# When the output weights of layer 0's attention are read and cut, and where the first output product and head 7's joins stand

## The chip, the cores and the metric

One core of one Trainium2 chip runs the whole program. The metric is device time in microseconds (us) of one execution, the median of several. Names of the engines: PE is TensorE (matrix products and transposes), PEld its weight loads, DVE is VectorE, ACT is ScalarE, POOL is GpSimd (nearly unused here), and SP only issues transfers (DMAs); SPq marks these issues. A `DMA_DIRECT2D` row is one issue; its transfer lands some microseconds later.

## The reference: what is computed

A decoder of two layers on x of 1024 tokens by 1024 columns, all in float32. Layer 0 mixes tokens by softmax attention in three groups of windows, layer 1 by gated linear attention; behind each stands an MLP with squared relu. The change lies in the end of layer 0's attention:

```python
def dilated_attention(h, w_in, w_out):
    qkv = (h @ w_in).reshape(B, S, N_GROUPS, 3, ATTN_HEADS, HEAD_DIM)
    for g, (window, dil) in enumerate(DILATED_GROUPS):   # 3 groups, 8 heads of 128
        q = apply_rope(qkv[:, :, g, 0], cos, sin) * (HEAD_DIM ** -0.5)
        k = apply_rope(qkv[:, :, g, 1], cos, sin)
        v = qkv[:, :, g, 2].astype(jnp.float32)
        o_g, lse_g = dilated_group_attention(q, k, v, dil, window // dil)
...
    alpha = jax.nn.softmax(jnp.stack(lses, axis=0), axis=0)
    o = jnp.sum(alpha[..., None] * jnp.stack(outs, axis=0), axis=0)
    return o.reshape(B, S, ATTN_WIDTH).astype(h.dtype) @ w_out
...
        x = x + dilated_attention(h, attn_w_in[j], attn_w_out[j])
```

Each head's three group outputs are merged by weights from the softmax denominators (here called a join); the eight heads side by side are multiplied by `w_out` (the output product), and x is added.

## The kernel before, in words

**Products.** Float32 matrices are held as two parts, a rounded high part and the rest (names ending in h or hi, and in l or lo). `mm3` (line 212) makes one product from three matmuls: high by high (L213), high by rest (L214), rest by high (L215). ACT casts the high part, and DVE subtracts it to get the rest (L222 for operands, L151 and L152 for weights).

**Weights.** The queue `W` holds the output product's weights in pieces of 128 by 1024 (512 KB) in the order in which they are needed. `W.dma()` (L132, its transfer L135) issues the load of the next piece (tile raw); `W.prep()` casts it (ACT `whi`, L151) and takes the rest (DVE `wlo`, L152). `W.pump()` (line 161) loads up to four pieces ahead and casts at most two of them, as long as `W.limit` plus the number of pieces given back lies above the number of casts. A piece needs a buffer of pool k4 (25 buffers) for raw, whi and wlo each.

**Attention.** There are 24 units p of one head and one group each, head by head. `run_head(p)` makes unit p's products (tiles pX, pY, pZ, pV) in 14 half products and calls `advance()` behind each: a clock goes on by one step, and all that `at(clock, function, rank)` has put down for that step is issued, in the order of the ranks. So `advance()` is what lays other work between products; the engines' queues then run in the order of issue. Unit p's rotary step is DVE work: c is added up from a bank (L1070), its halves are swapped by two copies (cw<-c, L1071 and L1072), and L1079, L1080 and L1087 give qT or kT. The attention of unit p runs while unit p + 1's products do: `scores` (PE pS, L976), `soft` (DVE L990, ACT's exponentials pt, L992), `turn` (PE's transposes pP, L1003, and ACT's copy L1005), `values` (PE pO, L1017). The result (orow) goes to a scratch og in HBM (L1024 or L1027).

**Joins.** `merge_load` reads the three groups' results of one head and of half of the tokens (rows, L1150). `merge_weights` and `merge` are DVE work (L1157 to L1175) and end in the tile om. Heads 0 to 6 write om to a scratch `oscr` in HBM, from where the output product's operand comes back: ol (heads 0 to 3, L1235) and ol2 (heads 4 to 6, L1434). Head 7's om is transposed by PE straight away (`t_head`, pT, L1218). Every operand is transposed (pT) and cut: heads 0 to 3 into oTh and oTl, heads 4 to 7 into o1h and o1l.

**The end of the attention.** With p = 23, the last unit, the output product's first four weights and ol are loaded and cast by hand-set clocks (c is the clock at the unit's start; lines 1406 to 1413). The last unit's own attention has no products of a following unit to stand between; `tail()` (line 1423) sets down its steps, the loads of ol2, the transposes of heads 4 to 6 and head 7's two joins by clock, advances three steps and leaves 40 more in the list `steps`.

**The output product.** `out_proj(0, ...)` (line 1448) runs over the 8 blocks of 128 tokens and 2 halves of the columns, first with the weights of heads 0 to 3, then with those of heads 4 to 7. `add_block` makes 12 matmuls into one of PE's 8 banks (pd), adds the residual xs (DVE, L1468) and calls `tick()`. In this stage each `tick()` takes two entries from `steps` and calls `W.pump()`:

```python
            xx = xs[tb // 2][:, tb % 2, 512 * n:512 * n + 512]
            dve.tensor_tensor(xx, ps, xx, op=OP.add)
            if quiet:
                W.pump()
            else:
                tick()
```

So a block of `add_block` is two steps of the clock, and what `tail()` has set down stands between the blocks.

Of the kernel before, what the change touches and what calls it, by code (L numbers as in the profile page):

```python
# [22 lines left out]
NB = S // P  # L23
# [18 lines left out]
def hybrid_trunk(ctx, tc, x, norm_mix, norm_mlp, norm_fin, a_in, a_out, g_in, g_up, g_b, g_nw,  # L42
# [32 lines left out]
    steps = deque()  # L75
# [104 lines left out]
    W = Weights()  # L180
# [104 lines left out]
    class Split:  # L285
# [4 lines left out]
        @staticmethod  # L290
        def at(tiles, k):
            n = 4 // len(tiles)
            return tiles[k // n][:, k % n, :]
# [11 lines left out]
    class Halves:  # L305
# [108 lines left out]
        def finish(self):  # L414
            up, a = self.up, self.a
            P1, P2, P6, P5, P7, P4, P3 = range(7)

            def split(name, src, lo):
                for c in range(2):
                    self.split(name, src, c, self.one, lo)  # L420

            up.product(0, P1)
            self.sum2(0)
            up.done(0, P1)
            up.first_stage(2)
            up.product(0, P2)
            up.stage(0, 3)
            up.product(1, P1)
            self.turn(3)
            up.first_stage(3)  # L430
            up.product(1, P2)
            up.product(2, P1)
            up.product(2, P2)
            up.product(3, P1)
            up.product(3, P2)
            up.done(1, P1)
            self.sum1(1)
            self.sum2(1)
            split("s2", self.s2, self.two)
            up.add(0, P2)  # L440
            up.add(1, P2)
            up.done(2, P1)
            split("s1", self.s1, self.one)
            up.squared(0, P2)
            up.stage(1, 2)
            up.stage(1, 3)
            up.squared(1, P2)
            up.product(0, P6)
            up.add(2, P2)
            up.done(3, P1)  # L450
            self.sum3()
            up.squared(2, P2)
            up.stage(0, 4)
            up.product(0, P5)
            split("s3", a[0, 0], self.two)
            up.done(0, P6)
            up.stage(0, 5)
            up.stage(0, 6)
            up.load(2)
            up.product(1, P6)  # L460
            up.add(3, P2)
            split("a22", a[1, 1], self.one)
            up.done(1, P6)
            up.squared(3, P2)
            up.stage(1, 4)
            up.product(1, P5)
            up.stage(1, 5)
            up.product(0, P7)
            up.done(0, P7)
            up.product(0, P4)  # L470
            up.stage(1, 6)
            up.stage(2, 2)
            up.stage(2, 3)
            self.sum4()
            up.load(3)
            up.add(0, P4)
            up.product(1, P7)
            up.done(1, P7)
            split("s4", a[0, 1], self.two)
            up.squared(0, P4)  # L480
            up.product(1, P4)
            up.add(1, P4)
            up.product(2, P6)
            up.stage(2, 4)
            up.squared(1, P4)
            up.done(2, P6)
            up.product(2, P5)
            up.stage(2, 5)
            up.stage(2, 6)
            up.product(0, P3)  # L490
            up.product(1, P3)
            up.add(0, P3)
            up.squared(0, P3)
            up.sums(0)
# [437 lines left out]
    clock = [0]  # L932
# [5 lines left out]
    def advance():  # L938
        clock[0] += 1
        for _, fn in sorted(agenda.pop(clock[0], []), key=lambda e: e[0]):  # L940
            fn()
# [281 lines left out]
    def merged(h, half, o):  # L1223
        if h < HEADS - 1:
            sp.dma_start(oscr[512 * half:512 * half + 512, HD * h:HD * h + HD].rearrange("(b p) c -> p b c", p=P), o)
        else:
            def last():
                t_head(h, half, o)
                reached.add((0, half))
            at(clock[0] + 3, last)  # L1230

    def ahead_h8(pairs):

        t = h8([P, 4, 512], F32, "ol")
        sp.dma_start(t, oscr[512 * pairs:512 * pairs + 512, 0:512].rearrange("(b p) c -> p b c", p=P))  # L1235
        return [t[:, 0:2, :], t[:, 2:4, :]]
# [33 lines left out]
    for p in range(NB // 2):  # L1270
        t = h8([P, 2, D], F32, "x0")
# [125 lines left out]
    ol = []  # L1397
    turned = Turned(ol, x[0])
    for p in range(heads.count):
        h, g = divmod(p, NG)  # L1400
        if g == 1 and h:
            plan_merges(h - 1, 14 * p)
        if p == heads.count - 1:
            for k in range(0, KT, 2):
                add_rows(a_out, k)
            c = 14 * p
            at(c + 3, lambda: (ol.extend(ahead_h8(0)), W.dma(), W.dma()), 0)
            at(c + 4, lambda: (W.dma(), W.dma()), 0)
            for t in (6, 8, 9, 10):
                at(c + t, lambda: W.prep(dve), 7)  # L1410
            at(c + 8, lambda: turned.turn(0), 7)
            at(c + 9, lambda: (turned.load_x(0), turned.load_x(1)))
            at(c + 11, lambda: turned.turn(1), 7)
            at(c + 17, lambda: ol.extend(ahead_h8(1)), 9)
        heads.run_head(p)
# [7 lines left out]
    def tail():  # L1423

        c = clock[0]
        heads.follow(heads.count - 1, c, ((6, 7, 8, 9), (9, 10, 11, 12), (11, 12, 13, 14)))
        load, start, finish = merges(HEADS - 1, merged)
        rows = {}
        for _ in range(3):
            advance()  # L1430

        def early(half):
            t = rows[half] = h8([P, 4, 512], F32, "ol2")
            sp.dma_start(t[:, :, 0:384], oscr[512 * half:512 * half + 512, 512:896].rearrange("(b p) c -> p b c", p=P))  # L1434
        at(c + 7, lambda: early(0))
        at(c + 16, lambda: early(1))
        for i, (half, h) in enumerate(((0, 4), (0, 5), (0, 6), (1, 4), (1, 5), (1, 6))):
            at(c + (13 + 3 * i if half == 0 else 21 + i), lambda half=half, h=h: t_head(h, half, rows[half][:, :, HD * (h - 4):HD * (h - 4) + HD]))
        at(c + 15, lambda: (load(0), load(1)), 9)
        at(c + 20, lambda: start(0))  # L1440
        at(c + 21, lambda: finish(0))
        at(c + 22, lambda: start(1))
        at(c + 23, lambda: finish(1))
        steps.extend([advance] * 40)

    tail()


    def out_proj(layer, wbc_row, o, up):
        oT, xs, load_x = o.t, o.xs, o.load_x  # L1450
        load_x(0)
        load_x(1)
        rate[0] = 2 - layer
        W.limit = 4
        o.turn(0)
        w = W.take(4)

        def add_block(tb, lhs, w, n, quiet=False):
            last = tb == NB - 1 and n == 1
            ps = bank("pd")  # L1460
            for k in range(4):
                a, b = lhs(k)
                wh, wl = w[k]
                mm3(ps, a, b, wh[:, 512 * n:512 * n + 512], wl[:, 512 * n:512 * n + 512], k == 0, k == 3)
                if last:
                    W.free(1)
            xx = xs[tb // 2][:, tb % 2, 512 * n:512 * n + 512]
            dve.tensor_tensor(xx, ps, xx, op=OP.add)  # L1468
            if quiet:
# [4 lines that stand above are left out]
        for tb in range(NB):  # L1474
            if tb % 2 == 0:
                o.turn(tb // 2 + 1)
                if layer and tb < 4:
                    o.o.append(ahead_k4(tb // 2 + 2))
            load_x(tb + 2)
            if tb == (NB - 4 if layer else 3):  # L1480
                W.limit = 6
            if tb == NB - 1 and layer:
                W.limit = 8
            for n in range(2):
                add_block(tb, lambda k: tuple(t[k // 2][:, k % 2, 128 * tb:128 * tb + 128] for t in oT), w, n, layer == 0 and tb == NB - 1 and n == 1)
        drain_to((layer, 0))
        W.limit = 5
        w = W.take(4)
        wbc = load_norm_w(wbc_row)
        st = Halves(xs, wbc, up, xmid)  # L1490
        for tb in range(NB):
            if tb == 2:
                drain_to((layer, 1))
            for n in range(2):
                if n:
                    st.middle(tb)
                add_block(tb, lambda k: tuple(t[:, k % 2, 128 * (tb % 4):128 * (tb % 4) + 128]
                                              for t in oT1[tb // 4, k // 2]), w, n)
            st.after(tb)
        oT1.clear()  # L1500
        rate[0] = 1
        st.finish()
# [488 lines left out]
    ol, turn1 = [], []  # L1991
# [6 lines left out]
    mid, last = slice(2 * RANK, 4 * RANK), slice(4 * RANK, 6 * RANK)  # L1998
# [74 lines left out]
```

## Time and profile before

| what | value |
|---|---|
| median of three runs | 2618.7 us (2617.86, 2618.7, 2620.56) |
| profiled execution, its own time | 2618.82 us |
| span in its trace | 2617.0 us |
| PE busy | 2590.2 us (99%) |
| DVE busy | 1859.8 us (71%) |
| ACT busy | 1277.1 us (49%) |
| POOL busy | 1.8 us |
| mean DMA rate | 162 GB/s |

The span is the time between the first and the last record of the trace; the profiled execution's own time is longer by what lies around it. A row of the trace's list by groups reads: start in the span, duration of one, engine, line, operation, out<-in by the names of the tiles (buffer numbers left out), their shapes, the count (the duration is then the mean of one), and in brackets the idle time of the engine ahead of it, with what ended that wait. The list of waits gives total, count and longest. A row by stretches gives length, then the busy time of PE, PEld, DVE, ACT and POOL with the count of instructions, then PE's granted clock (1.00 is full), the busy share of the DMA engines, and GB/s.

The change lies between 830 us and 930 us of this span: products of unit 23 up to 860.18 us, the output product with the first four weights up to 922.92 us; what is left of the last unit's attention stands between its blocks.

### The profile page before, as it was taken

Reading aid. Unit: us, or ns where it says so; the run is one execution under the profiler, and the core shown is the slowest. Engines: PE = TensorE matmul, PEld = TensorE weight load, DVE = VectorE, ACT = ScalarE, POOL = GpSimd, SP = SyncE. Lnnn points to the kernel's source line nnn. Section 1 sums busy time; section 2 is a strip of 40 time slices with the busy share of each in tenths; the row PEclk is TensorE's granted clock in tenths of the full one; section 3 lists DMA queues with packets and bytes.
Section 4 is the critical chain, followed back from the end, with each engine's and each line's share of the span. In section 5 each row is a group of like instructions: output and inputs, shape, how many; then the busy total and the mean of one; then the engine's idle time right before and its main releaser. Section 6 shows DMA issues by size and latency. Waiting matters only on the chain.

```text
span 2617.0 us, 33041 instructions
## 1 busy us (share of the span) xinstructions
PE 2590.2 (99%) x12144; PEld 2159.1 (83%) x12144; DVE 1859.8 (71%) x2986; ACT 1277.1 (49%) x2319; POOL 1.8 (0%) x7
## 2 busy tenths in 40 slices
PE   8999999999999999999999999999999999999998
PEld 6888888888888888888888888778888888888887
DVE  7645888888888768666657587877658866666566
ACT  6333455555555436555534345654326555553343
POOL 0000000000000000000000000000000000000000
PEclk9999999999999999999999999999999999999999
DMA  5534365655656733544775452462523544396543
GB/s 189 169 129 125 101 162 133 163 151 145 160 148 172 232 121 111 179 160 146 268 263 185 139 196 96 127 205 97 176 72 127 170 147 163 127 355 202 187 147 125
DMA packets 327010, 423.12 MB, mean 162 GB/s; under 512 B 19808, under 2 KB 192224, under 8 KB 326848
## 3 DMA queue, kind: packets, MB, share of 16 engines
q1 hardware_dynamic: 326848, 421.01, 51.0%
q8 instruction: 95, 1.56, 0.2%
q14 instruction: 67, 0.55, 0.1%
HBM read 279.71 MB, written 116.06 MB: 151 GB/s over the span
## 4 chain that ended last, share of the span: by engine, by line
PE 88%; DVE 7%; ACT 3%; issue 1%; DMA 1%; SPq 0%; ACTq 0%; DVEq 0%
PE pX L598 17%; PE pB L1578 13%; PE pV L598 11%; PE pA L1578 10%; PE pY L598 6%; PE pZ L598 6%; PE pB L829 5%; PE pd L215 3%; PE pd L214 3%; PE pd L213 3%; PE pA L829 3%; PE pS L976 2%; PE pO L1017 2%; DVE dl L814 1%; PE pP L1003 1%
## 5 line engine op out<-in xcount | busy, mean ns | idle before, releaser
L1578 PE MATMUL pB<-dh 128*128 128x512 f32 x512 | 199.4, 389 | 0.0
L1578 PE MATMUL pB<-dh,dl 128*128 128x512 f32 x512 | 199.2, 389 | 0.0
L1578 PE MATMUL pB<-dl,dh 128*128 128x512 f32 x512 | 199.2, 389 | 0.0
L222 DVE TENSOR_TENSOR dl<-sin,dh 128x1024 fp32r<-128x1024 f32 x112 | 136.5, 1219 | 45.9 <-ACT dh L219 45.3
L219 ACT ACTIVATE dh<-sin 128x1024 fp32r<-128x1024 f32 x112 | 117.9, 1052 | 91.0 <-PE pB L1578 32.2
L219 ACT ACTIVATE dh<-kept 128x1024 fp32r<-128x1024 f32 x64 | 67.9, 1061 | 182.5 <-DVE kept L1543 137.8
L598 PE MATMUL pV<-s4h,wd 128*128 128x512 f32 x448 | 150.8, 398 | 0.0
L1578 PE MATMUL pA<-dh,dl 128*128 128x512 f32 x384 | 149.4, 389 | 0.0
L1578 PE MATMUL pA<-dh 128*128 128x512 f32 x384 | 149.4, 389 | 0.0
L1578 PE MATMUL pA<-dl,dh 128*128 128x512 f32 x384 | 149.4, 389 | 0.0
L992 ACT ACTIVATE pt<-pt,orow 128x128 f32<-128x128 f32 (+1 forms) x192 | 84.8, 442 | 96.7 <-DVE orow L990 96.7
L1578 PEld LDWEIGHTS pB<-dl,dh 128*128 128x128 f32 x512 | 96.1, 188 | 20.0
L1578 PEld LDWEIGHTS pB<-dh,dl 128*128 128x128 f32 x512 | 96.1, 188 | 19.9
L1578 PEld LDWEIGHTS pB<-dh 128*128 128x128 f32 x512 | 96.1, 188 | 19.8
L536 DVE TENSOR_TENSOR wal<-raw,wah 128x512 fp32r<-128x512 f32 x112 | 76.2, 687 | 42.9 <-ACT wah L535 42.9
L607 ACT ACTIVATE c<-c 128x512 f32<-128x512 f32 x64 | 40.4, 632 | 122.7 <-DVE c L635 78.9
L598 PEld LDWEIGHTS pV<-s4h,wd 128*128 128x128 f32 x448 | 84.1, 188 | 17.8 <-DVE rb L623 0.3
L536 DVE TENSOR_TENSOR wbl<-t,wbh 128x1024 fp32r<-128x1024 f32 x56 | 68.6, 1225 | 38.4 <-ACT wbh L535 38.4
L222 DVE TENSOR_TENSOR dl<-kept,dh 128x1024 fp32r<-128x1024 f32 x64 | 78.3, 1224 | 24.5 <-ACT dh L219 18.6
L990 DVE CUSTOM_DVE_ANT_0 pt<-pS,masks 128x128 f32<-128x128 f32 (+1 forms) x192 | 58.2, 347 | 50.5 <-PE pS L976 50.5
L598 PE MATMUL pY<-a12h,wah 128*128 128x512 f32 x224 | 89.5, 400 | 0.0
L598 PE MATMUL pZ<-a22h,wgh 128*128 128x512 f32 x224 | 89.3, 399 | 0.0
(336 smaller groups left out, 7370.5 us busy)
## 6 DMA issues: line engine op xcount, KB each, us to landing
sin<-acts SPq DMA_DIRECT2D x112, 512.0 KB, 3.9
raw<-in_mlp_w_up_dram SPq DMA_DIRECT2D x64, 512.0 KB, 5.8
acts<-s SPq DMA_DIRECT2D x64, 512.0 KB, 3.4
raw<-in_mlp_w_down_dram SPq DMA_DIRECT2D x64, 512.0 KB, 4.7
raw<-in_attn_w_in_dram SPq DMA_DIRECT2D x96, 256.0 KB, 4.5
cw<-c SPq DMA_DIRECT2D x192, 128.0 KB, 2.3
acts<-c SPq DMA_DIRECT2D x64, 256.0 KB, 2.1
kept<-in_mlp_w_down_dram SPq DMA_DIRECT2D x32, 512.0 KB, 5.7
```

The costliest lines, as they stand in the source:

```text
L213: pe.matmul(ps, sh, mh, start=start, stop=False)
L214: pe.matmul(ps, sh, ml, start=False, stop=False)
L215: pe.matmul(ps, sl, mh, start=False, stop=stop)
L219: act.activation(hi, src, AF.Copy)
L222: dve.tensor_tensor(lo, src, hi.bitcast(F32), op=OP.subtract)
L536: self.remain(lambda: dve.tensor_tensor(lo, src, hi.bitcast(F32), op=OP.subtract))
L598: pe.matmul(st[b], u[:, k, :], v, start=first and k + n == 0, stop=k == 3 and n == 2, skip_group_check=True)
L829: pe.matmul(self.acc[s][t], a[:, c], b[:, k, :], start=fresh and m + k + v == 0, stop=m == 1 and k == 1 and v == 2, skip_group_check=True)
L976: pe.matmul(ps[:, i, :128 * n], self.qT[:, 128 * b:128 * b + 128], self.kT[:, k0:k0 + 128 * n], start=True, stop=True)
L990: dve.tensor_tensor_reduce(pt[:, i, :128 * n], ps[:, i, :128 * n], masks[:, m0:m0 + 128 * n], -scale, 1e38, op0=OP.add, op1=OP.min, accum_ ...
L992: act.activation(pt[:, i, :128 * n], pt[:, i, :128 * n], AF.Exp, scale=-1.0, bias=m, accum_out=self.row[:, r, HD:HD + 1])
L1578: pe.matmul(self.acc[s][t], a[:, k, c], b[:, k, :], start=fresh and m + k + v == 0, stop=m == 7 and k == 1 and v == 2, skip_group_check=True)
```

## The change

```diff
@@ merged
-            at(clock[0] + 3, last)
+            at(clock[0] + 7, last)
@@ the last unit
-            at(c + 3, lambda: (ol.extend(ahead_h8(0)), W.dma(), W.dma()), 0)
-            at(c + 4, lambda: (W.dma(), W.dma()), 0)
-            for t in (6, 8, 9, 10):
+            at(c + 1, lambda: (W.dma(), W.dma()), 0)
+            at(c + 2, lambda: (W.dma(), W.dma()), 0)
+            at(c + 3, lambda: ol.extend(ahead_h8(0)), 0)
+            for t in (5, 6, 7, 8):
                 at(c + t, lambda: W.prep(dve), 7)
@@ tail
-        for _ in range(3):
-            advance()
+        advance()
...
-        at(c + 20, lambda: start(0))
-        at(c + 21, lambda: finish(0))
-        at(c + 22, lambda: start(1))
-        at(c + 23, lambda: finish(1))
-        steps.extend([advance] * 40)
+        at(c + 18, lambda: start(0))
+        at(c + 19, lambda: finish(0))
+        at(c + 20, lambda: start(1))
+        at(c + 21, lambda: finish(1))
+        steps.extend([advance] * 42)
@@ out_proj
-        def add_block(tb, lhs, w, n, quiet=False):
+        def add_block(tb, lhs, w, n, quiet=False, woven=False):
...
                 if last:
                     W.free(1)
+                if woven and k % 2:
+                    steps.popleft()()
...
-            if tb == NB - 1 and layer:
+            if tb == NB - 1:
                 W.limit = 8
             for n in range(2):
-                add_block(tb, ..., w, n, layer == 0 and tb == NB - 1 and n == 1)
+                add_block(tb, ..., w, n,
+                          layer == 0 and tb == NB - 1 and n == 1, layer == 0 and tb + n == 0)
```

The loads of the four weights stand two clock steps sooner and ahead of ol; their casts stand at steps 5 to 8 instead of 6, 8, 9 and 10. One step of the last unit's attention instead of three runs ahead of the output product, and two run inside its first block, behind its sixth and its twelfth matmul. Head 7's joins stand two steps sooner, and the transposes of their results four steps further behind. At the last block of the first weights `W.limit` is 8 in layer 0 as well. Nothing is added or left out: every engine has the same instructions in another order. Behind line 1466 the changed kernel's line numbers are larger by 2 or 3.

On SP, at the start of the last unit (raw is a weight's load, cw<-c the two copies of the rotary step, og the last results but one, ol the operand of heads 0 to 3):

```order
 L1072 DMA cw<-c 64x512
-L1071 DMA cw<-c 64x512
-L1072 DMA cw<-c 64x512
+L135 DMA raw<-in_attn_w_out_dram 128x1024 x2
+L1071 DMA cw<-c 64x512
+L1072 DMA cw<-c 64x512
+L135 DMA raw<-in_attn_w_out_dram 128x1024 x2
 L1024 DMA og_78<-orow 128x4x130
 L1235 DMA ol<-oscr 128x4x512
-L135 DMA raw<-in_attn_w_out_dram 128x1024 x4
```

The four loads, which stood behind ol, are in two pairs now, one ahead of the second pair of copies and one behind it; ol is behind all of them.

On PE, at the end of the last unit's attention and the start of the output product, before (pP are transposes of the exponentials, pO the values' products, pd the output product):

```order
L1003 MATMUL pP_7791<-ident_68,pt_7729 128x128 x3
L1017 MATMUL pO_7796<-v_7635,pt_7685 128x128 x3
L1003 MATMUL pP_7814<-ident_68,pt_7776 128x128 x3
L1017 MATMUL pO_7796<-v_7635,pt_7729 128x128 x3
L213 MATMUL pd_7831<-whi_7638,oTh_1901 128x512
L214 MATMUL pd_7831<-wlo_7639,oTh_1901 128x512
```

and in the changed kernel:

```order
L1003 MATMUL pP_7791<-ident_68,pt_7729 128x128 x3
L1017 MATMUL pO_7796<-v_7639,pt_7693 128x128 x3
L213 MATMUL pd_7815<-whi_7623,oTh_1901 128x512
L214 MATMUL pd_7815<-wlo_7624,oTh_1901 128x512
L215 MATMUL pd_7815<-whi_7623,oTl_1903 128x512
L213 MATMUL pd_7815<-whi_7642,oTh_1901 128x512
L214 MATMUL pd_7815<-wlo_7643,oTh_1901 128x512
L215 MATMUL pd_7815<-whi_7642,oTl_1903 128x512
L1003 MATMUL pP_7822<-ident_68,pt_7776 128x128 x3
L1017 MATMUL pO_7796<-v_7639,pt_7729 128x128 x3
```

Six matmuls of the first block stand between two attention steps, ahead of the second group of transposes.

On DVE, inside the output product, before (xs is a block's residual add, o1l and oTl rests of transposed operands, mz to om head 7's joins):

```order
L1468 TENSOR_TENSOR xs<-pd,xs 128x512
L222 TENSOR_TENSOR o1l<-pT,o1h 128x512
L222 TENSOR_TENSOR oTl<-pT,oTh 128x2x256 x2
L1468 TENSOR_TENSOR xs<-pd,xs 128x512
L1157 TENSOR_REDUCE mz<-rows 128x4
L1158 TENSOR_TENSOR md<-mz,rows 128x12
```

and in the changed kernel:

```order
L1470 TENSOR_TENSOR xs<-pd,xs 128x512
L1157 TENSOR_REDUCE mz<-rows 128x4
L1158 TENSOR_TENSOR md<-mz,rows 128x12
L222 TENSOR_TENSOR o1l<-pT,o1h 128x512
L1163 TENSOR_TENSOR md<-me,rows 128x12
L1164 TENSOR_REDUCE mz<-md 128x4
L1165 RECIPROCAL mz<-mz 128x4
L1166 TENSOR_TENSOR me<-me,mz 128x12
L1181 TENSOR_TENSOR rows<-rows,me 128x12x128
L1174 TENSOR_TENSOR om<-rows 128x512
L1175 TENSOR_TENSOR om<-om,rows 128x512
L222 TENSOR_TENSOR oTl<-pT,oTh 128x2x256 x2
```

The first join begins one block sooner, and it stands ahead of two rests (oTl) and of an add that it stood behind.

More of the change, by code (lines that the diff above doesn't have):

```diff
@@ L1481, in out_proj @@
                 W.limit = 6
-            if tb == NB - 1 and layer:
+            if tb == NB - 1:
                 W.limit = 8
             for n in range(2):
-                add_block(tb, lambda k: tuple(t[k // 2][:, k % 2, 128 * tb:128 * tb + 128] for t in oT), w, n, layer == 0 and tb == NB - 1 and n == 1)
+                add_block(tb, lambda k: tuple(t[k // 2][:, k % 2, 128 * tb:128 * tb + 128] for t in oT), w, n,
+                          layer == 0 and tb == NB - 1 and n == 1, layer == 0 and tb + n == 0)
         drain_to((layer, 0))
```

## The prediction

> **What bounds the kernel now.** I read the page first, then PE's waits in the stretch that the diff touches, then that stretch in time, engine by engine.
>
> The page's first rows give the span and the busy time of each engine.
>
> ```profile
> span 2617.0 us, 33041 instructions
> PE 2590.2 (99%) x12144; PEld 2159.1 (83%) x12144; DVE 1859.8 (71%) x2986; ACT 1277.1 (49%) x2319; POOL 1.8 (0%) x7
> ```
>
> PE sets the time almost everywhere: all that it is not busy comes to 27 us. The matmuls of layer 0's output product stay the same in number, so the change can only gain where PE stands still or runs slowly. This is who PE waited for from 845 to 930 us (total, times, longest).
>
> ```profile
> PE pP L1003 <- ACT pt L992: 1.2, 2, 1.1
> PE pT L1218 <- DVE om L1175: 0.6, 1, 0.6
> PE pd L214 <- DVE wlo L152: 0.5, 2, 0.3
> PE pO L1017 <- ACT pt L1005: 0.2, 1, 0.2
> ```
>
> Three places: the exponentials of the last attention steps, the join of head 7 (om), and the rests (wlo) of two late weights. The first costs more than its wait, which the stretches show (length, then busy us of PE, PEld, DVE, ACT and POOL, then granted clock, DMA share, GB/s).
>
> ```profile
> 833.00:839.00 6.00, 6.00 (x39) 5.31 (x38) 5.86 (x16) 5.00 (x16) 0.00 (x0) 1.00 0.31 68
> 861.00:864.43 3.43, 2.04 (x13) 1.25 (x11) 3.37 (x13) 2.41 (x9) 0.00 (x0) 1.00 0.26 55
> 864.43:867.84 3.41, 3.41 (x11) 2.98 (x12) 3.38 (x5) 1.72 (x6) 0.00 (x0) 0.50 0.60 141
> ```
>
> PE works 2.04 of 3.43 us, and then has half its clock for 3.41 us: 1.7 us lost on top. DVE meanwhile is full (3.37 of 3.43). So the question here is why DVE is late.
>
> **The first part: weights sooner, product between the steps.** DVE's rows from 848 us, idle time in brackets, with ACT's first weight cast and the issue of the weights on SP behind them.
>
> ```profile
> 848.63 1.23 DVE L152 TENSOR_TENSOR wlo<-raw,whi 128x1024 fp32r<-128x1024 f32 x1 [1.74 <-ACT whi L151]
> 850.06 1.23 DVE L152 TENSOR_TENSOR wlo<-raw,whi 128x1024 fp32r<-128x1024 f32 x1 [0.21 <-ACT whi L151]
> ...
> 853.42 0.69 DVE L1079 TENSOR_TENSOR cw<-cw,tab 128x512 f32<-128x512 f32 x1 [0.38 <-DMA cw<-c]
> ...
> 860.60 1.29 DVE L222 TENSOR_TENSOR oTl<-pT,oTh 128x512 fp32r<-128x512 f32 x2 [1.25 <-ACT oTh L219]
> ...
> 869.70 0.69 DVE L1468 TENSOR_TENSOR xs<-pd,xs 128x512 f32<-128x512 f32 x1 [0.52 <-PE pd L215]
> ...
> 871.62 1.16 DVE L1087 TENSOR_TENSOR qT<-c,cw 128x512 f32<-128x512 f32 x1
> ```
> ```profile
> 847.53 1.06 ACT L151 ACTIVATE whi<-raw 128x1024 fp32r<-128x1024 f32 x1 [3.47 <-DMA raw<-in_attn_w_out_dram]
> ```
> ```profile
> 832.50 0.59 SPq L1072 DMA_DIRECT2D cw<-c  x1
> ...
> 839.14 0.50 SPq L1235 DMA_DIRECT2D ol<-oscr  x1
> 839.70 2.45 SPq L135 DMA_DIRECT2D raw<-in_attn_w_out_dram  x4
> ```
>
> DVE's idle times here are 1.74 + 0.21 + 0.38 + 1.25 + 0.52 = 4.10 us. The first two are the weights': issued from 839.70, in a queue that is full by then. In the change two of them go out behind the copies at 832.50 and two behind the next pair, into a queue that was 0.31 busy. By four transfers of 512 KB that land 7.8 to 9.9 us after issues 2 us apart,
>
> ```profile
> DMA to landing us min/median/max: 7.8/8.9/9.9
> ```
>
> one takes (851.6 - 847.5)/3 = 1.37 us, so I estimate all four to be in by 843, before ACT asks at about 844. That takes out 1.95 us. The 0.38 (a copy that stood behind the four weights) goes too. The 1.25 stays: ACT does the exponentials first, and those wait for DVE. The 0.52 goes, since the product's first block no longer ends late. DVE is 2.85 us sooner; but its c from pZ can't run before PE's pZ ends, which takes back up to 0.15. qT, which ended at 871.62 + 1.16 = 872.78, ends at about 870.0.
>
> PE, in the same stretch:
>
> ```profile
> 848.50 1.04 PE L259 MATMUL pT<-ident,ol 128*128 128x128 f32 x8
> ...
> 863.49 0.33 PE L1003 MATMUL pP<-ident,pt 128*128 128x128 f32 x1 [1.07 <-ACT pt L992]
> 864.35 1.61 PE L1017 MATMUL pO<-v,pt 128*128 128x128 f32 x6
> ...
> 872.77 0.39 PE L214 MATMUL pd<-wlo,oTh 128*128 128x512 f32 x1
> 873.00 0.39 PE L215 MATMUL pd<-whi,oTl 128*128 128x512 f32 x1
> 873.23 0.60 PE L976 MATMUL pS<-kT,qT 128*128 128x128 f32 x4
> ```
>
> Six matmuls of the product, at 0.23 us each (872.77 to 873.00) 1.4 us of work, now stand ahead of the pP that waited 1.07. With DVE 2.3 us sooner there, the exponentials are early by more than that: the waits (1.2 + 0.2 = 1.4 in the list above) and the half clock (1.7) both go, 3.1 us and the restarts behind them. PE could reach pS of the last group at about 869.8; qT's end holds it to 870.0 or 870.1. **First term: 873.23 - 870.05 = 3.2 us.** DVE sets it: the weave alone would be worth what DVE waited for PE behind the half clock, 0.52 us, and the weights alone nearly all. Its ends: 3.3 if pZ holds nothing up, and 0.9 if only the 0.52 and PE's slack of 0.45 behind qT come out.
>
> What pays: ol goes out behind the last two weights. It landed at 846.2,
>
> ```profile
> DMA to landing us min/median/max: 7.0/7.0/7.0
> ```
>
> and PE takes it at 848.50. Two weights ahead of it are at most 2 x 1.37 = 2.7 us: 848.9 at the latest, so PE waits 0 to 0.4 us. I keep 0.3; it is within the 0.15 above, since PE has time to spare there until qT.
>
> [...]
>
> **The next operand.** PE being 3.2 us sooner, the next transfer is nearly late: head 4 to 6's rows (ol2, issued at 876.11).
>
> ```profile
> 866.63 0.90 SPq L1027 DMA_DIRECT2D og<-orow  x2
> ...
> 876.11 0.46 SPq L1434 DMA_DIRECT2D ol<-oscr  x1
> ```
> ```profile
> DMA to landing us min/median/max: 10.3/10.3/10.3
> ```
> ```profile
> 887.07 0.60 PE L1218 MATMUL pT<-ident,ol 128*128 128x128 f32 x4
> ```
>
> It landed at 886.4, and PE would now ask at 883.9. The queue is full up to there, so ol2 comes sooner by what starts sooner: one xs transfer (1.37 us) moves ahead of og into an idle queue, and og, behind values at 864.35, I put 1.0 us sooner (values came at half clock). 886.4 - 2.4 = 884.0 to 884.2. **Second term: -0.25 us**, with 0 and 2.5 (it lands as before) as its ends.
>
> **Joins and transposes.** DVE makes head 7's two joins from 901.53 on; PE's last transposes wait for the second.
>
> ```profile
> 901.53 0.17 DVE L1157 TENSOR_REDUCE mz<-rows 128x4 f32<-128x12 f32 x1
> ...
> 910.76 0.69 DVE L1175 TENSOR_TENSOR om<-om,rows 128x512 f32<-128x512 f32 x1
> ```
> ```profile
> 911.50 0.66 PE L1218 MATMUL pT<-ident,om 128*128 128x128 f32 x4 [0.65 <-DVE om L1175]
> ```
>
> The wait is 0.65 us, and a restart as below (0.16): 0.81 lost. Four steps are two blocks, so it goes. But the joins (9.9 us of DVE, from 901.53 to 910.76 + 0.69) now stand ahead of oTl and of the xs adds that free PE's banks, and they begin one block after the load of their rows instead of two: DVE may stand for those rows, and the adds come late. With eight banks in turn I estimate a wait of 0 to 0.4 us from that. **Third term: 0.81 - 0.2 = 0.6 us**, from 0.4 to 0.8.
>
> **The limit of 8 in layer 0.** The last two wlo move ahead of the product's last add.
>
> ```profile
> 924.28 0.39 PE L213 MATMUL pd<-whi,o1h 128*128 128x512 f32 x1
> 925.00 0.50 PE L214 MATMUL pd<-wlo,o1h 128*128 128x512 f32 x1 [0.33 <-DVE wlo L152]
> ...
> 925.57 0.40 PE L213 MATMUL pd<-whi,o1h 128*128 128x512 f32 x1
> 926.14 0.50 PE L214 MATMUL pd<-wlo,o1h 128*128 128x512 f32 x1 [0.17 <-DVE wlo L152]
> ```
>
> Two steps take 0.72 and 0.57 us instead of 0.23 (the first: 0.33 idle and 0.16 of restart). **Fourth term: 0.49 + 0.34 = 0.83 us**, from the bare idle time, 0.5, to 1.05 if the steps behind them pay too. DVE's 2.4 us for the two are the same; the product's last blocks hide them, and if they didn't, the adds behind them would hold PE's banks, at most as long as now.
>
> **Sum.** 3.2 - 0.25 + 0.6 + 0.83 = 4.4 us. Behind 930 us every engine's order is as before and PE nearly never waits, so what is gained there stays. The profiled execution took 2618.82 us, which is the median of the three runs (2618.7; 2617.86 to 2620.56) within 0.1: 2618.7 - 4.4 = **2614.3 us**.
>
> **Rivals.**
> - ol2 lands as before, because its queue is full whatever starts first: PE waits 2.5 us at 884. 3.2 - 2.5 + 0.6 + 0.83 = 2.1: 2616.6 us. For it: that queue is backed up by 10.3 us. Against: what is ahead of ol2 starts sooner.
> - The clock halves all the same. The stretch that brought it is now filled by small transposes and six product matmuls; if they don't suffice, 1.7 us are back: 2616.0 us. For it: PE was busy 2.04 of 3.43 us, not idle, and was throttled even so. Against: without waits it is full. [...]
> - The weights don't land sooner, since SP must wait for buffers that PE frees (the order shows such a wait on both pairs). Then DVE's 1.95 and 0.38 stay and the first term is 0.9: 2616.6 us. Against: the same four tiles, out of the same 25 buffers, were issued within 2.45 us at 839.70.
> [...]
> - Slower: joins begun on rows that aren't there. DVE stands, with oTl and the adds queued behind; PE runs out of banks and loses 1 us per 1 us. These are the issue and the landing of the two halves' rows:
>
> ```profile
> 894.75 0.91 SPq L1150 DMA_DIRECT2D rows<-og  x2
> ```
> ```profile
> DMA to landing us min/median/max: 4.8/5.6/6.4
> ```
>
> The first landed at 899.5; I expect it at about 897, since it follows PE's last values. The gain of 4.4 is used up if it lands past 901.4. At 904, which takes five more transfers of 1.37 us ahead of it, the time is 2621.3 us. Against: PE's values, their copy out and this load all move together.
>
> **How the numbers follow.** Forecast 0.66, ol2 0.11, clock 0.08, weights 0.05, ol 0.05, slower 0.05. The terms' upper ends give 3.3 + 0 + 0.8 + 1.05 = 5.2; with runs that differ from their median by about 1 us, the low end is 2618.7 - 5.2 - 1 = 2612.5. The upper end takes in the first four rivals and the same 1 us: 2618.2. A measurement of this kernel tells about 0.2%, or 5.2 us, from no change: faster means under 2613.5, which only the upper ends of the forecast reach (0.26); slower than 2623.9 takes the last rival worse than I priced it (0.04); the rest, 0.70, is within.
>
> **What would show it.** In the changed profile: no idle time of DVE before its first wlo; a granted clock of 1.00 from 861 to 868; pS of the last group near 870.0 behind a short wait for qT; a wait of some tenths for ol and ol2; no PE wait for om and none for wlo near 920. Wrong would be a wait of over 1 us at one of the transposes, or half clock at a new place.

## The result and the profile after

The changed kernel takes 2613.15 us (median of 12 runs, 2612.59 to 2614.78) against 2618.55 us before (median of 12, 2617.22 to 2620.56): a ratio of 0.998, 95% interval 0.9973 to 0.9988, so 5.4 us sooner with 3.1 to 7.1 us as the interval. The forecast was 2614.3 us in a range of 2612.5 to 2618.2.

The page's first rows, of the changed kernel's profiled execution (it took 2613.06 us):

```profile
span 2611.3 us, 33042 instructions
PE 2586.3 (99%) x12144; PEld 2157.3 (83%) x12144; DVE 1858.9 (71%) x2986; ACT 1276.7 (49%) x2319; POOL 1.8 (0%) x7
```

PE's busy time fell by 3.9 us although it has the same instructions. A half clock counts as busy time (3.41 of 3.41 us at 864.43 before), and it is gone, but that is 1.7 us at most. The rest isn't traced: two later profiles of the kernel before, at full clock, have 2587.7 and 2588.9 us (e9 and e10 below), so this figure differs by over a microsecond between executions of one kernel. The list of PE's waits from 828 to 932 us, which had four rows before, now has its heading alone. The stretches where PE stood still before are full (columns as in the prediction):

```profile
862.00:868.00 6.00, 6.00 (x37) 5.17 (x36) 5.90 (x9) 1.99 (x5) 0.00 (x0) 1.00 0.75 203
...
910.00:916.00 6.00, 6.00 (x28) 4.94 (x27) 4.16 (x8) 2.49 (x3) 0.00 (x0) 1.00 0.00 0
916.00:922.00 6.00, 6.00 (x28) 4.97 (x27) 3.78 (x5) 0.00 (x0) 0.00 (x0) 1.00 0.27 89
```

SP's rows, from the last but one pair of copies to ol, and ol2's issue, with the landing of the two operands behind them:

```profile
832.82 1.08 SPq L135 DMA_DIRECT2D raw<-in_attn_w_out_dram  x2
...
837.10 1.61 SPq L135 DMA_DIRECT2D raw<-in_attn_w_out_dram  x2
...
839.28 0.45 SPq L1235 DMA_DIRECT2D ol<-oscr  x1
...
872.29 0.37 SPq L1434 DMA_DIRECT2D ol<-oscr  x1
```
```profile
DMA to landing us min/median/max: 8.4/8.4/8.4
```
```profile
DMA to landing us min/median/max: 9.8/9.8/9.8
```

So ol is in at 847.7 and ol2 at 882.1 us. DVE's rows:

```profile
845.14 1.23 DVE L152 TENSOR_TENSOR wlo<-raw,whi 128x1024 fp32r<-128x1024 f32 x1
...
847.61 3.49 DVE L152 TENSOR_TENSOR wlo<-raw,whi 128x1024 fp32r<-128x1024 f32 x3
...
857.55 1.29 DVE L222 TENSOR_TENSOR oTl<-pT,oTh 128x512 fp32r<-128x512 f32 x2 [1.19 <-ACT oTh L219]
...
866.02 0.70 DVE L1470 TENSOR_TENSOR xs<-pd,xs 128x512 f32<-128x512 f32 x1
866.62 0.69 DVE L1079 TENSOR_TENSOR cw<-cw,tab 128x512 f32<-128x512 f32 x1
...
867.95 1.20 DVE L1087 TENSOR_TENSOR qT<-c,cw 128x512 f32<-128x512 f32 x1
...
895.50 0.17 DVE L1157 TENSOR_REDUCE mz<-rows 128x4 f32<-128x12 f32 x1 [0.84 <-DMA rows<-og]
```

Of the five idle times of before only the one ahead of oTl is left (1.19 us), and a new one of 0.84 stands ahead of the first join, whose rows are not in yet. Last PE, at the places that the prediction named:

```profile
848.18 1.04 PE L259 MATMUL pT<-ident,ol 128*128 128x128 f32 x8
...
869.21 0.71 PE L976 MATMUL pS<-kT,qT 128*128 128x128 f32 x4
...
870.43 0.61 PE L976 MATMUL pS<-kT,qT 128*128 128x128 f32 x4
...
883.11 0.60 PE L1218 MATMUL pT<-ident,ol 128*128 128x128 f32 x4
...
909.43 0.60 PE L1218 MATMUL pT<-ident,om 128*128 128x128 f32 x4
...
918.05 0.39 PE L213 MATMUL pd<-whi,o1h 128*128 128x512 f32 x1
```

None of them has a bracket: ol was 0.5 us early (847.7 for 848.18), ol2 1.0 us (882.1 for 883.11).

**A measure that does not hang on the start of the span.** Executions of the same instructions differ already ahead of the change: the first of the rows below starts at 841.74 us in e3 and at 843.23 in e9, whose order is the same up to there. I therefore measure between four instructions of PE. In the profile before they are:

```profile
842.31 0.48 PE L598 MATMUL pV<-s1h,wbh 128*128 128x512 f32 x1
...
874.34 0.61 PE L976 MATMUL pS<-kT,qT 128*128 128x128 f32 x4
...
922.92 0.39 PE L213 MATMUL pd<-whi,o1h 128*128 128x512 f32 x1
...
929.43 0.39 PE L213 MATMUL pd<-whi,o1h 128*128 128x512 f32 x1
```

Stretch 1 runs from the first pV matmul behind the values at 840 us to the second pS of the last group (all of the weights and of the weave), stretch 2 to the first o1h matmul (ol2, the joins and their transposes), stretch 3 to the first matmul of the third o1h block, 24 matmuls on (the last weights). In all kernels below PE executes the same work in each of the three. Each figure is of one profiled execution; where the instructions are the same and the clock is full, such figures differ by up to 0.5 us in stretch 1 (30.44 to 30.94) and by up to 0.06 in stretches 2 and 3.

| kernel | stretch 1 | stretch 2 | stretch 3 | sum | median of the runs |
|---|---|---|---|---|---|
| before | 32.03 | 48.58 | 6.51 | 87.12 | 2618.55 |
| changed | 28.44 | 47.62 | 5.44 | 81.50 | 2613.15 |
| difference | -3.59 | -0.96 | -1.07 | -5.62 | -5.4 |

### The profile page after: what moved, and what is told of

The parts are those of the page before. It is cut to its first block, busy times and chain, and to the rows that moved or that the text cites. A ratio compares the mean times of both kernels' runs of the same rounds, so it can differ in the third digit from the quotient of the medians.

```text
span 2611.3 us, 33042 instructions
## 1 busy us (share of the span) xinstructions
PE 2586.3 (99%) x12144; PEld 2157.3 (83%) x12144; DVE 1858.9 (71%) x2986; ACT 1276.7 (49%) x2319; POOL 1.8 (0%) x7
## 4 chain that ended last, share of the span: by engine, by line
PE 87%; DVE 8%; ACT 3%; issue 1%; DMA 1%; SPq 0%; ACTq 0%; DVEq 0%
PE pX L598 16%; PE pB L1581 13%; PE pV L598 11%; PE pA L1581 10%; PE pY L598 5%; PE pZ L598 5%; PE pB L829 5%; PE pd L215 3%; PE pd L213 3%; PE pd L214 3%; PE pA L829 3%; PE pO L1017 2%; PE pS L976 2%; PE pP L1003 1%; DVE dl L814 1%
```

## The experiments

**The four parts alone.** Each has one part of the diff on the kernel before (its main lines; left out are e3's clocks and, in e2, the new argument of `add_block` and the 42 steps instead of 40).

```diff
 # e1: weights
-            at(c + 3, lambda: (ol.extend(ahead_h8(0)), W.dma(), W.dma()), 0)
-            at(c + 4, lambda: (W.dma(), W.dma()), 0)
-            for t in (6, 8, 9, 10):
+            at(c + 1, lambda: (W.dma(), W.dma()), 0)
+            at(c + 2, lambda: (W.dma(), W.dma()), 0)
+            at(c + 3, lambda: ol.extend(ahead_h8(0)), 0)
+            for t in (5, 6, 7, 8):
 # e2: weave
-        for _ in range(3):
-            advance()
+        advance()
...
+                if woven and k % 2:
+                    steps.popleft()()
 # e3: joins at c + 18 to 21, and
-            at(clock[0] + 3, last)
+            at(clock[0] + 7, last)
 # e4: limit
-            if tb == NB - 1 and layer:
+            if tb == NB - 1:
```

> The kernel before with the weights' part of the change alone (loads at steps 1 and 2, ol behind them, casts at steps 5 to 8). Theory A (DVE sets the first stretch): DVE loses its idle times 1.74, 0.21 and 0.38 us and about 0.1 us of restart behind each, so qT is about 2.7 to 3.2 us sooner, PE's wait for the exponentials (1.2 us) and the half clock at 864 us go without the weave, and the time is 3.0 us below before, 2615.5 us. Theory B (PE must be filled by the weave): the waits and the half clock stay, only the queue in front of them moves, and the time is at most 1.0 us below before.

> The kernel before with the product's first block woven between the last attention steps, and nothing else. Theory A: DVE still makes qT at about 872.3 us, so PE waits there for qT what it gained ahead of it: 0.5 us below before, 2618.0 us; PE's wait moves from pP to pS. Theory B: six matmuls of 0.23 us stand ahead of the pP that waited 1.07 us, wait and half clock go, 3.1 us below before, 2615.4 us.

> The kernel before with head 7's joins two steps sooner and their transposes four further behind, and nothing else. Theory A: PE's wait for om (0.65 us) and its restart go, and the regrouped transposes save about 0.1: 0.8 to 0.95 us below before, 2617.7 us, though DVE stands for the rows for some tenths. Rival: DVE's wait for the rows makes the adds late and PE waits for banks: within 0.3 us of before.

> The kernel before with the limit of 8 in layer 0 as well, and nothing else. Theory A: the two waits for wlo (0.33 and 0.17 us) go with their restarts, 1.05 us in all behind 922 us: 2617.5 us. Rival: the casts ahead of the last add only move the wait to a bank: within 0.3 us of before.

Measured (the runs of before beside these four have a median of 2617.97 us):

| kernel | stretch 1 | stretch 2 | stretch 3 | median | ratio, interval |
|---|---|---|---|---|---|
| e1, weights | 28.48 | 48.53 | 6.53 | 2615.3 | 0.999 (0.9982 to 0.9999) |
| e2, weave | 31.42 | 48.58 | 6.53 | 2618.69 | 1.0003 (0.9994 to 1.0011) |
| e3, joins | 30.94 | 47.67 | 6.53 | 2616.47 | 0.9997 (0.9988 to 1.0006) |
| e4, limit | 30.81 | 48.56 | 5.44 | 2616.69 | 0.9996 (0.9988 to 1.0005) |

The intervals of e2, e3 and e4 include no change, so their medians alone don't tell what those parts are worth; the stretches do. Each part does its work in its own stretch and in no other. Theory A holds against B: the weights alone bring stretch 1 to 28.48, where the whole change has 28.44. The weave alone moves PE's wait, as A said, but the 0.5 us that A gave it did not come. From e2, the longest wait in PE's list, its row, and DVE's qT ahead of it:

```profile
PE pS L976 <- DVE mz L1157: 1.9, 1, 1.9
```
```profile
872.96 0.68 PE L976 MATMUL pS<-kT,qT 128*128 128x128 f32 x4 [1.89 <-DVE mz L1157]
```
```profile
871.74 1.08 DVE L1087 TENSOR_TENSOR qT<-c,cw 128x512 f32<-128x512 f32 x1
```

The list names mz, but pS takes qT, which ends at 872.82, 0.14 us ahead of it. The wait of pP for the exponentials is gone, and 1.89 us of waiting for qT stand in its place.

One thing fits neither theory: e3 and e4 have the order of before up to 873 us, and their stretch 1 is 1.1 to 1.2 us shorter. Their granted clock is 1.00 from 861 to 870 us.

**The kernel before, profiled again.** So the unchanged kernel was profiled twice more.

> The kernel before, unchanged, profiled a second time. Theory H (the half clock at 864 us belonged to the one execution that was profiled; the experiments with joins or limit alone, which have the same order up to 873 us, had full clock there): full clock at 861 to 868 us, PE waits 1.2 us for the exponentials all the same, 0.4 to 0.5 us for qT, and pS of the last group is about 1.2 us sooner against the instructions ahead of 830 us. Rival (the half clock is this kernel's own): half clock for 3.4 us again.

> As the run ahead of it: theory H expects full clock in this execution too, or in most; the rival half clock in each.

Both had full clock. This is the third profile (e10): PE's waits, and two stretches of 3.41 us laid as the half clock lay in the first.

```profile
PE pP L1003 <- ACT pt L992: 1.2, 2, 1.1
...
PE pS L976 <- DVE mz L1157: 0.5, 1, 0.5
```
```profile
861.00:864.41 3.41, 2.17 (x14) 1.49 (x13) 3.35 (x11) 2.39 (x9) 0.00 (x0) 1.00 0.26 56
864.41:867.82 3.41, 3.41 (x19) 2.85 (x18) 3.38 (x7) 1.79 (x7) 0.00 (x0) 1.00 0.74 173
```
```profile
863.66 0.33 PE L1003 MATMUL pP<-ident,pt 128*128 128x128 f32 x1 [1.07 <-ACT pt L992]
864.15 0.44 PE L1003 MATMUL pP<-ident,pt 128*128 128x128 f32 x2 [0.17 <-ACT pt L992]
```

| kernel | stretch 1 | stretch 2 | stretch 3 | clock at 861 to 870 us |
|---|---|---|---|---|
| before, first profile | 32.03 | 48.58 | 6.51 | half for 3.41 us |
| e9 | 30.44 | 48.59 | 6.53 | full |
| e10 | 30.91 | 48.57 | 6.51 | full |

The same wait of 1.07 us at the same instruction, and no half clock behind it. Theory H holds: of five executions with this order up to 873 us (before, e3, e4, e9, e10) one had it; the wait is 1.07 us in four of them and 0.76 in e9. Without the half clock stretch 1 is 30.44 to 30.94, 30.78 in the mean. So it costs about 1.25 us (1.1 to 1.6), not the 1.7 lost while it lasts, since PE then waits 0.5 us less for qT.

Runs without a profile have a trace of it too: the mean granted clock over the span, given to three places for each run. It is 0.998 in the two profiled executions with a half clock inside the work (before, and e6 below) and 0.999 in the eleven without. Of the 81 runs of before that stand beside the experiments 10 have 0.998 (median 2618.38 us) and 71 have 0.999 (2617.75 us). The changed kernel has 0.999 in all its 12 runs, and so have e1, e3, e4, e5, e7, e8 and e11 in all of theirs; e2 has 0.998 in 3 of 11. Where in the span such a run lost its clock the mean doesn't tell.

**Loads without the casts.** e11 moves the loads and leaves the casts where they were.

```diff
-            at(c + 3, lambda: (ol.extend(ahead_h8(0)), W.dma(), W.dma()), 0)
-            at(c + 4, lambda: (W.dma(), W.dma()), 0)
+            at(c + 1, lambda: (W.dma(), W.dma()), 0)
+            at(c + 2, lambda: (W.dma(), W.dma()), 0)
+            at(c + 3, lambda: ol.extend(ahead_h8(0)), 0)
```

> The kernel before with the weights' loads at steps 1 and 2 and ol behind them, the casts at their old steps (6, 8, 9, 10). If DVE's idle time came from the landings alone, this has the whole gain of the weights: pS of the last group near 869.6 us on the clock of the profile before, 2.4 us sooner than without a half clock, and no idle time of DVE before a wlo. If the casts' steps matter, DVE's idle times stay in part and the gain is under 1.5 us.

Stretch 1 is 29.26 us: of the 2.3 us that the weights bring (30.78 to 28.48) the loads alone bring about 1.5, and the casts' steps the other 0.8. The median was 2615.84 us (2618.06 before; 0.9993, 0.9984 to 1.0002). No idle time stands ahead of a wlo any more, so the landings explain those; but one of 0.57 us is left ahead of the first oTl, which waits for ACT:

```profile
849.50 1.29 DVE L222 TENSOR_TENSOR oTl<-pT,oTh 128x512 fp32r<-128x512 f32 x2 [0.57 <-ACT oTh L219]
```

**The change without the weave** (e5: the diff without its lines of e2).

> The changed kernel without the weave (three steps ahead of the product again). Theory A: DVE sets the first stretch, and the weave adds at most the 0.5 us that DVE waits for the first block: 2613.2 to 2613.7 us, full clock at 862 to 868 us. Theory B: the wait for the exponentials and the half clock come back, 2.5 to 3 us: 2616 us.

Stretches of 28.46, 47.67 and 5.44 us, and 2613.2 us (2617.93 before; 0.9981, 0.9972 to 0.999): the times of the changed kernel, without one of its four edits. The clock is full at 861 to 870 us. Theory A.

**Four weights ahead of ol.** e6 is the changed kernel with this:

```diff
-            at(c + 1, lambda: (W.dma(), W.dma()), 0)
-            at(c + 2, lambda: (W.dma(), W.dma()), 0)
-            at(c + 3, lambda: ol.extend(ahead_h8(0)), 0)
+            at(c + 3, lambda: (W.dma(), W.dma(), W.dma(), W.dma(), ol.extend(ahead_h8(0))), 0)
```

> The changed kernel with all four weights issued in one go at step 3, straight ahead of ol; casts as in the change. Theory R (what is issued ahead delays what is behind): four times 1.37 us stand ahead of ol, it lands at about 851 to 852 us, PE waits 3.0 to 3.5 us for it, and the time is about 2616.5 us. Rival (transfers run beside each other): ol lands by 849 us, PE waits under 0.7 us for it, and only DVE's idle time ahead of the casts (about 2.3 us) comes back: 2615.4 us.

The issues, ol's landing, PE's row, and the stretch behind that wait:

```profile
839.60 1.95 SPq L135 DMA_DIRECT2D raw<-in_attn_w_out_dram  x4
841.64 0.57 SPq L1235 DMA_DIRECT2D ol<-oscr  x1
```
```profile
DMA to landing us min/median/max: 10.3/10.3/10.3
```
```profile
852.09 1.06 PE L259 MATMUL pT<-ident,ol 128*128 128x128 f32 x8 [2.97 <-DMA ol<-oscr]
```
```profile
853.40:856.81 3.41, 3.41 (x9) 2.64 (x9) 3.38 (x9) 1.92 (x6) 0.00 (x0) 0.50 1.13 351
```

ol lands at 841.64 + 10.3 = 851.9 us, where theory R had it, and PE waits 2.97 us. Stretch 1 is 33.15, 4.7 us longer than in the change: 3.0 of waiting and 1.7 of a half clock behind it, 3.41 us long again. The median was 2617.37 us (1.0, 0.9991 to 1.0009): this order gives up what the other edits bring. Not every run of it has the half clock: three of its 11 have a mean clock of 0.999 and took 2615.74 to 2615.98 us, the eight at 0.998 took 2616.96 to 2621.44. So the wait alone costs about 2.7 us against the changed kernel's 2613.15.

**Joins sooner still.** e7 is the changed kernel with the joins at c + 16 to c + 19 and `at(clock[0] + 9, last)`.

> The changed kernel with the joins two steps sooner still (steps 16 to 19) and their transposes where the change has them. DVE then waits about 5 us for the rows, with rests, two weights and adds queued behind. Theory S (the slower rival of the prediction): PE runs out of banks or operands and loses most of that, 3 to 5 us: 2616 to 2618 us. Rival (eight banks and operands made early hide it): 2613.2 us, and no wait of PE above 0.3 us.

DVE's wait for the rows, and PE's two waits that come of it:

```profile
895.12 0.17 DVE L1157 TENSOR_REDUCE mz<-rows 128x4 f32<-128x12 f32 x1 [3.33 <-DMA rows<-og]
```
```profile
904.52 0.50 PE L213 MATMUL pd<-whi,oTh 128*128 128x512 f32 x1 [0.92 <-DVE o1l L222]
...
909.07 0.66 PE L1218 MATMUL pT<-ident,ol 128*128 128x128 f32 x4 [1.57 <-DVE oTl L222]
```

Theory S: stretch 2 is 51.06 us, 3.44 longer than in the change, for a wait of 3.33; 2616.65 us (0.9994, 0.9986 to 1.0003). About 5 us of waiting were expected. The 0.84 us that DVE waits in the changed kernel bring no wait of PE.

**Transposes in larger groups.** e8 is the changed kernel with this:

```diff
-            at(c + (13 + 3 * i if half == 0 else 21 + i), ...)
+            at(c + (16 if half == 0 and i < 2 else 19 if half == 0 else 24), ...)
```

> The changed kernel with the transposes of heads 4 to 6 in larger groups: heads 4 and 5 of the first half of the tokens at one step, and all three of the second half at one step. If PE pays about 0.13 us whenever it goes from product to transposes and back, the start of the o1h product comes 0.2 to 0.4 us sooner (too little for the time itself to tell); if it doesn't, it stays. If the cuts of the larger groups come late, PE waits for a bank or an operand and it is later.

28.46, 47.68 and 5.44 us, 2613.13 us (0.9982, 0.9973 to 0.999): nothing changes. Grouping saves nothing here, and the rows show why: four transposes take 0.36 us up to the next matmul, eight 0.79 and twelve 1.23, so each four more in a group take 0.43 or 0.44, which uses up what the matmul behind a group saves (it takes 0.31 or 0.32 us instead of 0.23).

## Why the prediction was right, and where it was not

The forecast lies 1.2 us above the measured median, inside its range. The median also lies under the 2613.5 us that the prediction called faster, a case to which it gave 0.26 against 0.70 for no clear change. The forecast's sum was 4.4 us. The trace gives 5.62 us against the first profile of before, and 81.50 against 30.78 + 48.58 + 6.52 = 85.88, so 4.4 us, against an execution without the half clock. That the sum agrees is luck: the first term is 0.9 us too large, and the other three together are 0.85 us too small.

- **First term, 3.2 us: mechanism right, size wrong.** DVE sets it, the weights bring nearly all of it, and the casts' idle times were what paid: e1, e2 and e5 show that. The step that failed is "PE ... then has half its clock for 3.41 us", taken as a standing part of the kernel, along with DVE's 0.52 us, which came from it. Without a half clock stretch 1 gains 30.78 - 28.44 = 2.3 us; against the first profile 3.59. The 2.3 is close to DVE's idle times that the weights take away: 1.7 to 2.1 us in e3, e4, e9 and e10 (the 0.38 for the copy is there in e10 alone, as 0.33), and some 0.1 us more for each restart. "The weave alone would be worth ... 0.52 us" is refuted: without a half clock DVE doesn't wait for that block, and the weave is worth nothing measurable, alone (31.42 against 30.44 to 30.94; e2's DVE is late ahead of the weave already: its second pair of oTl begins 18.50 us behind stretch 1's start, e10's 18.04, e9's 17.55) or in the change (28.46 without it, 28.44 with it).
- **What hides behind a restart.** An idle time in brackets is less than what it costs: DVE's rows at 866.02 and 866.62 are 0.60 us apart with 0.70 us of duration, so a row without a wait begins 0.1 us before the end of the one ahead. I counted that for PE (0.16) but not for DVE.
- **ol: the wait was 0, within the 0 to 0.4 that were put.** It took 8.4 us to landing where it was 7.0. The first two weights had landed by 838.1 us, ahead of ol's issue at 839.28, so two stood ahead of it, as the prediction had it. e6 shows the cliff beside it: behind all four weights it costs 3 us and, in 8 of 11 runs, a half clock.
- **Second term, -0.25: it was 0.** ol2 was issued 3.8 us sooner and landed 4.3 sooner (before: 876.11 and 886.4). The failed step is "og ... I put 1.0 us sooner": the values ahead of og ended at 864.05 instead of 865.96 us, and og was issued at 864.72 instead of 866.63, 1.9 us sooner. With the 1.37 of the xs transfer, which did move ahead of og, that gives 3.3 of the 4.3; the rest isn't traced.
- **Third term, 0.6: it was 0.96.** The 0.81 was right; the 0.2 taken off for DVE standing for the rows was not due, for DVE stood 0.84 us and no wait of PE followed. e3 alone gives 48.58 - 47.67 = 0.91. About 0.1 more than the wait and its restart I can't place; e8 speaks against the grouping of the transposes.
- **Fourth term, 0.83: it was 1.07.** The upper end (1.05): the step behind each late wlo pays too, 0.34 us where 0.23 is usual.
- **Rivals.** ol2 landing as before, late weights and a late ol did not come. The range's upper end, 2618.2 us, takes in a time of 2617.2 us for a late ol (the chance of 0.05). No run of the changed kernel shows such a delay: ol landed at 847.7 us and PE did not wait for it. In e6, which puts all four weights straight ahead of ol, PE waits 2.97 us for it, and the median is 2617.37 us. The slower rival's mechanism exists (e7: 3.44 us lost for 3.33 us of waiting), but in the changed kernel DVE takes the rows at 895.50 us, far ahead of 901.4, after 0.84 us of waiting.
- **The clock rival** was asked the wrong way round: whether the half clock would stay, instead of whether it had been there in other executions. Both half clocks lasted 3.41 us (before and e6), a wait of 0.76 to 1.07 us at the same place brought one in one of five executions, and by the mean clocks above 10 of 81 runs of before had one. What decides in which execution it comes, no run shows.

What PE must lack for the clock to halve stays open. In before PE is busy 2.02 us in the 3.41 us ahead of the half clock (861.02 to 864.43); e10 has 2.17 us in the stretch laid alike (861.00 to 864.41, shown above) and full clock behind it. But busy time alone doesn't decide. These are stretches of e2 and of e7 with less, and the clock stays full behind both (the mean clock of either profiled execution is 0.999):

```profile
871.55:874.96 3.41, 2.00 (x16) 1.99 (x17) 3.11 (x13) 0.82 (x3) 0.00 (x0) 1.00 1.04 336
```
```profile
906.45:909.86 3.41, 1.84 (x11) 1.17 (x10) 3.34 (x6) 0.04 (x1) 0.00 (x0) 1.00 0.00 0
```

The clock rival asked whether small transposes fill the stretch. In this one near the start of e5 all of PE's 2.48 busy us are transposes (L334), and the clock is full in it and behind it, while in the changed kernel 3.42 us without any work of PE (2603.65 to 2607.07 us, at the end) are followed by a granted clock of 0.50:

```profile
35.13:38.54 3.41, 2.48 (x16) 1.77 (x17) 3.41 (x6) 1.68 (x3) 0.00 (x0) 1.00 0.00 0
38.54:41.96 3.42, 3.42 (x16) 2.55 (x16) 3.32 (x5) 2.83 (x6) 0.00 (x0) 1.00 0.00 0
```

How much of the 5.4 us is the half clock? The interval of 3.1 to 7.1 takes in both 4.4 and 5.6, but the later runs say that it is little: the changed kernel lies 4.6 us under the 71 runs of before with a mean clock of 0.999 (which did not run beside it), and e5 and e8 lie 4.7 and 4.8 us under the 2617.93 beside them. The 12 runs of before beside the result have a median 0.5 to 0.6 us above the later ones (2617.93 to 2618.06). Why, stays open: of their clocks only the profiled one is on record.

## What to carry to other kernels

Before you count a clock drop of one profile as a cost, profile the same kernel again, or look at the mean granted clock of its other runs: a drop that follows a gap of about 1 us may be that execution's alone (here it came in one of five, behind a wait of 1.07 us), and a sum made against it is too large by it. Where an engine waits in front of its last input, ask who makes that input: filling the waiting engine (the weave) only moved the wait to qT, while taking the idle times out of DVE's queue moved the whole stretch. And a load that is put ahead of another has a cliff: two 512 KB transfers ahead of ol were free, four cost 4.7 us in the profiled execution.

## What the runs showed of the hardware

Inside the work the granted clock halved for 3.41 us at a time, in before (864.43 to 867.84 us) and in e6 (853.40 to 856.81 us) alike. Behind a stretch of 3.41 us in which PE was busy 2.02 us it halved in before; behind 2.17 us in e10, at the same place, it did not, and neither did it behind 2.00 us in e2 or 1.84 us in e7. With a single wait of 2.97 us (e6) it halved in the profiled execution, and 8 of 11 runs have the mean clock of 0.998 that goes with it; before has it in 10 of 81. In a stretch of nothing but transposes, PE busy 2.48 of 3.41 us (e5), the clock was full, and it was full behind it.

The more 512 KB weights still stood ahead of ol on SP's queue, the later it landed behind its issue: 7.0 us with none, 8.4 with two, 10.3 with four.
